# One step of a chunked RWKV-7 scan: four small products on the two column halves of TensorE

## The chip, the cores and the metric

The kernel runs on one core of a Trainium2 chip. The metric is the time of one execution on the device, in microseconds (us). Before the change the median of three executions is 3085.67 us. In the profile, PE is TensorE's products and PEld its weight loads, DVE is VectorE, ACT is ScalarE, POOL is GpSimd and SP the queue of SyncE, which here only issues transfers.

## The reference

The model is two layers. Each is a half-step feed-forward block, a mixer and a second half-step feed-forward block, at width 1024 over 528 tokens (16 learned tokens and 512 of the input). The mixer runs a convolution branch beside an RWKV-7 branch of 16 heads of size 64. The change lies in the recurrence of that branch, which the reference writes token by token:

```python
def _rwkv7_scan(r, decay, k, v, kk, a):
    B, L, H, N = r.shape
    ...
    def step(S, inp):
        r_t, w_t, k_t, v_t, kk_t, a_t = inp
        sa = jnp.einsum("bhvk,bhk->bhv", S, -kk_t)
        S = (S * w_t[:, :, None, :]
             + sa[..., None] * (kk_t * a_t)[:, :, None, :]
             + v_t[..., None] * k_t[:, :, None, :])
        y = jnp.einsum("bhvk,bhk->bhv", S, r_t)
        return S, y
    S0 = jnp.zeros((B, H, N, N), jnp.float32)
    _, ys = lax.scan(step, S0, xs)
    return jnp.moveaxis(ys, 0, 1)
```

## The kernel before, in words

**The chunked scan.** The 512 tokens are cut into eight chunks of 64 (`NCH` = 8, `C` = 64), and the 16 heads into four groups of four. `scan` (L1389) handles one group, with one pass of its loop for each chunk, so there are 2 x 4 x 8 = 64 scan steps in the program. Within a step the four heads h = 0 to 3 are handled side by side, and a step needs the state that the step before it left.

**One step.** Two transposes (L1404) bring the values of the chunk into rows 0 to 63 of the PSUM tile `tr`. ScalarE copies them into rows 0 to 63 of `sv` (L1405), whose rows 64 to 127 already hold the state, and into rows 0 to 63 of `va` (L1407). Four products (L1409), one for each head, take the whole 128 rows of `sv[:, h]` against 64 columns of `G`, the array that holds the masked scores above the decayed keys. They write 64 x 64 results side by side into columns 256 to 511 of `tr`, all in rows 0 to 63. ScalarE copies all four to `w` in one instruction of 64 x 256 (L1411). Then come two lists of products, head by head and in turn: L1418 multiplies `w` by the inverse that `inverse` put into `G`, into rows 64 to 127 of `ch`; L1421 multiplies the state by the decayed r, into rows 0 to 63. Each works on one 64 x 64 quarter of the array. ScalarE copies L1418's result to `va` (L1424), four products of 128 x 128 (L1426) add the chunk's contribution, VectorE makes the next state (L1432, L1433), and ScalarE stores the output rows (L1439).

**Passes.** Each product of float32 operands stands in the trace as two weight loads and two passes, so L1409's four products are eight passes in a step. The products of the large projections (L246, L217) use float32r and are one pass each.

**What stands around the step.** While the scan runs, the mixer lays other work between its parts: projections for later groups (L246, each weight block against two halves of the tokens), the scores of the next group (transposes L1250, products L1259 of 64 rows by 128 columns, L1236 of 64 rows by 16 columns), the inverse of the next half (L1333 and L1340, on quarters of the array), transposes and output work of the group before (L1528), and on VectorE the taps of the convolution (L1088). The order in which the code calls these is not the order in which they run: a scheduler takes the recorded instructions, their dependences and priorities, and its own estimates of durations, and writes one list for each engine. Each engine then works its list strictly in order, so a change of one group's shape shifts what stands behind it. A few lists are tied together by hand: `chain` in `scan` fixes the order of L1418, L1421 and L1426 among themselves.

Of the kernel before, what the change touches and what calls it, by code (L numbers as in the profile page):

```python
# [16 lines left out]
P = 128  # L17
# [13 lines left out]
C = 64  # L31
# [67 lines left out]
class Trunk:  # L99
# [1289 lines left out]
    def scan(self, q, Q):  # L1389


        nc, mp = self.nc, self.mp
        G, SB, pc, sv = Q["G"], self.sb, Q["pc"], Q["sv"]
        hc = lambda x: x.rearrange("p (h v) -> p h v", h=4)
        ysb = mp.tile([P, NCH * 4, 32], F32, name="b4", bufs=B4)
        ysb = ysb.rearrange("p a b -> p (a b)").rearrange("p (m h v) -> p m h v", m=4, h=4)
        Q["y"] = ysb
        for c in range(NCH):
            cs = slice(NM + c * C, NM + (c + 1) * C)
            left = lambda h: slice(h * HS, (h + 1) * HS)  # L1400
            right = lambda h: slice(256 + h * HS, 256 + (h + 1) * HS)
            tr = self.sm("tr")
            for p in range(2):
                nc.tensor.transpose(tr[0:C, p * P:(p + 1) * P], Q["v"][p][:, cs], self.ident)  # L1404
            nc.scalar.copy(sv[0:C], hc(tr[0:C, 0:256]))  # L1405
            va, w = (mp.tile([P, 4, HS], F32, name=x, bufs=n) for x, n in (("va", 2), ("w0", W0)))
            nc.scalar.copy(va[0:C], hc(tr[0:C, 0:256]))  # L1407
            for h in range(4):
                nc.tensor.matmul(tr[0:C, right(h)], G[:, h // 2, h % 2, 0, cs], sv[:, h, :],  # L1409
                                 start=True, stop=True)  # L1410
            nc.scalar.copy(w[0:C], hc(tr[0:C, 256:512]))  # L1411


            ch = self.sm("ch")
            chain = []
            rows = slice(0, P if c + 1 < NCH else C)
            for h in range(4):
                chain.append(nc.tensor.matmul(ch[C:P, left(h)], G[0:C, h // 2, h % 2, 1, cs],  # L1418
                                              w[0:C, h, :], start=h == 0, stop=True,
                                              skip_group_check=True))  # L1420
                chain.append(nc.tensor.matmul(ch[0:C, right(h)], G[HS:P, h // 2, h % 2, 1, cs],  # L1421
                                              sv[HS:P, h, :], start=h == 0, stop=False,
                                              skip_group_check=True))
            nc.scalar.copy(va[C:P], hc(ch[C:P, 0:256]))  # L1424
            for h in range(4):
                chain.append(nc.tensor.matmul(ch[rows, right(h)], SB[:, c, h, rows], va[:, h, :],  # L1426
                                              start=False, stop=True, skip_group_check=True))
            self.scanned = chain[-1]
            nsv = None
            if c + 1 < NCH:  # L1430
                nsv = self.new_state()
                nc.vector.tensor_tensor(nsv[HS:P], hc(ch[HS:P, 256:512]), sv[HS:P], op=ALU.add)  # L1432
                nc.vector.tensor_tensor(nsv[HS:P], nsv[HS:P],  # L1433
                                        pc[HS:P, :, c + 1:c + 2].to_broadcast([HS, 4, HS]),
                                        op=ALU.mult)
            for later, earlier in zip(chain[1:], chain):
                self.nosync(later, earlier)
            ro = C * (c % 2)
            nc.scalar.copy(ysb[ro:ro + C, c // 2], hc(ch[0:C, 256:512]))  # L1439
            sv = nsv  # L1440
            yield
# [317 lines left out]
```

## Time and profile before

| | |
|---|---|
| median of three executions | 3085.67 us (3079.16 to 3091.76) |
| the profiled execution | 3085.23 us |
| its span, first to last instruction | 3083.5 us |
| mean granted TensorE clock | 0.979 |
| scan steps, first and last copy to `w` | 64, from 622.6 to 2532.7 us |
| ScalarE busy | 1435.6 us (47%) |
| VectorE busy | 2277.9 us (74%) |

The page gives the busy time of each engine and a chain of work followed back from the last instruction. A row of a timeline has the start, the length, the engine, the line, the operation, what it writes and reads, and how many instructions were merged into the row. A row of a group has the count, the busy time and the mean duration, and then the idle time ahead of it and what ended that idle time. A row of waits has the waiting engine and line, what ended the wait, the total, the number of waits and the longest. The duration of a PE pass includes the way through the array, so what counts for throughput is the distance between starts, not the duration.

### The profile page before, as it was taken

The numbers are of one execution on the slowest core, as the hardware profiler recorded it, in microseconds if no ns is written. First come the engines' busy times: TensorE is split into PE (matmuls) and PEld (weight loads), VectorE is DVE, ScalarE is ACT, GpSimd is POOL, SyncE is SP. The second block draws the span as 40 slices with busy tenths as digits, with TensorE's granted clock in tenths as the row PEclk, the third lists the DMA queues.
The fourth block names the chain that finished last, engine by engine and source line by source line (L and its number), as shares of the span: only waits on it lengthen the run. The fifth ranks groups of instructions, "written<-read, shape, count | busy, mean of one in ns | idle before, by whom it ended". The sixth has DMA issues, their size and how long they took to land.

```text
span 3083.5 us, 64248 instructions
## 1 busy us (share of the span) xinstructions
PE 3009.6 (98%) x26140; PEld 2885.9 (94%) x26140; DVE 2277.9 (74%) x4689; ACT 1435.6 (47%) x2553; POOL 178.4 (6%) x286
## 2 busy tenths in 40 slices
PE   9999999999999999999999999999999999999998
PEld 9999999889988899999999999899889889999998
DVE  6766777897875768676776768778788757677767
ACT  4454454344454535444454544543354545254543
POOL 0110000000000000100000100000000000001100
PEclk9999999998999999999999999999899999999999
DMA  7665444334355554565556554444254645546651
GB/s 197 154 143 131 107 150 139 93 86 124 98 148 130 168 150 127 133 151 124 128 130 151 140 131 103 157 133 106 69 131 115 146 122 168 154 123 146 151 142 59
DMA packets 556149, 405.29 MB, mean 131 GB/s; under 512 B 89306, under 2 KB 500798, under 8 KB 555854
## 3 DMA queue, kind: packets, MB, share of 16 engines
q1 hardware_dynamic: 520302, 308.49, 34.9%
q0 software_dynamic: 30944, 84.18, 14.8%
q10 hardware_dynamic: 4608, 8.52, 0.8%
q8 instruction: 205, 3.36, 0.5%
q14 instruction: 90, 0.74, 0.1%
HBM read 270.81 MB, written 47.12 MB: 103 GB/s over the span
## 4 chain that ended last, share of the span: by engine, by line
PE 83%; DVE 7%; DMA 4%; ACT 3%; issue 2%; SPq 1%; ACTq 0%; DVEq 0%; POOLq 0%
PE mm L217 52%; PE mm L246 16%; PE sc L1340 2%; PE ch L1426 2%; PE tr L1409 1%; PE sc L1259 1%; PE ch L1418 1%; DMA w_raw<-in_w_in_dram 1%; DVE w_lo L160 1%; DVE cacc L1088 1%; ACT w_hi L149 1%; PE sc L1012 1%; DVE ln_rstd L444 1%; DMA w_lo<-w_raw 1%; PE sc L1144 1%
## 5 line engine op out<-in xcount | busy, mean ns | idle before, releaser
L217 PE MATMUL mm<-xh,w_hi 128*128 128x264 f32 (+1 forms) x1792 | 509.0, 285 | 7.6 <-ACT xh L460 5.7
L217 PE MATMUL mm<-xl,w_hi 128*128 128x264 f32 (+1 forms) x1792 | 507.8, 284 | 0.7 <-DVE xl L461 0.3
L217 PE MATMUL mm<-xh,w_lo 128*128 128x264 f32 (+1 forms) x1792 | 506.6, 283 | 0.0
L217 PE MATMUL mm<-hh,w_hi 128*128 128x264 f32 (+1 forms) x1408 | 400.4, 285 | 1.8 <-ACT hh L112 1.8
L217 PE MATMUL mm<-hh,w_lo 128*128 128x264 f32 (+1 forms) x1408 | 400.5, 285 | 0.0
L217 PE MATMUL mm<-hl,w_hi 128*128 128x264 f32 (+1 forms) x1408 | 400.1, 284 | 0.2
L246 PE MATMUL mm<-xh,w_lo 128*128 128x264 f32 x1760 | 390.3, 298 | 7.8 <-DMA w_lo<-w_raw 7.2
L246 PE MATMUL mm<-xh,w_hi 128*128 128x264 f32 x1760 | 385.8, 297 | 5.7 <-DVE kp L962 2.9
L246 PE MATMUL mm<-xl,w_hi 128*128 128x264 f32 x1760 | 385.0, 296 | 0.0
L1088 DVE SCALAR_TENSOR_TENSOR cacc<-cu,cw,cacc 128x528 f32<-128x528 f32 (+1 forms) x480 | 355.6, 752 | 4.3 <-ACT cacc L1086 0.6
L217 PEld LDWEIGHTS mm<-xh,w_hi 128*128 128x128 f32 x1792 | 335.9, 188 | 11.6 <-ACT xh L460 8.3
L217 PEld LDWEIGHTS mm<-xl,w_hi 128*128 128x128 f32 x1792 | 337.7, 189 | 2.7 <-DVE xl L461 2.5
L217 PEld LDWEIGHTS mm<-xh,w_lo 128*128 128x128 f32 x1792 | 337.5, 188 | 0.2 <-DVE w_lo L160 0.2
L122 ACT CAST w_hi<-sums 128x512 fp32r<-128x512 f32 (+1 forms) x204 | 154.7, 759 | 313.6 <-PE mm L217 202.1
L246 PEld LDWEIGHTS mm<-xh,w_lo 128*128 128x128 f32 x1760 | 285.0, 194 | 15.3 <-DMA w_lo<-w_raw 8.3
L246 PEld LDWEIGHTS mm<-xh,w_hi 128*128 128x128 f32 x1760 | 284.8, 194 | 12.1 <-DVE kp L962 3.2
L246 PEld LDWEIGHTS mm<-xl,w_hi 128*128 128x128 f32 x1760 | 283.8, 193 | 5.5
L217 PEld LDWEIGHTS mm<-hh,w_hi 128*128 128x128 f32 x1408 | 265.5, 189 | 2.4 <-ACT hh L112 2.0
L217 PEld LDWEIGHTS mm<-hl,w_hi 128*128 128x128 f32 x1408 | 265.7, 189 | 0.9 <-DVE hl L113 0.8
L217 PEld LDWEIGHTS mm<-hh,w_lo 128*128 128x128 f32 x1408 | 266.2, 189 | 0.1
L160 DVE TENSOR_TENSOR w_lo<-w_raw,w_hi 128x1024 fp32r<-128x1024 f32 (+1 forms) x194 | 204.1, 1054 | 80.8 <-ACT w_hi L149 72.1
L149 ACT CAST w_hi<-w_raw 128x1024 fp32r<-128x1024 f32 x134 | 140.4, 1049 | 240.3 <-PE mm L246 65.3
(364 smaller groups left out, 6847.1 us busy)
## 6 DMA issues: line engine op xcount, KB each, us to landing
w_raw<-in_w_in_dram SPq DMA_DIRECT2D x116, 512.0 KB
w_lo<-w_raw POOLq DMA_DIRECT2D x100, 512.0 KB, 5.0
w_raw<-in_ffn_wg_dram SPq DMA_DIRECT2D x88, 512.0 KB
w_raw<-in_ffn_wu_dram SPq DMA_DIRECT2D x88, 512.0 KB
w_raw<-in_ffn_wd_dram SPq DMA_DIRECT2D x80, 512.0 KB
w_lo<-w_raw POOLq DMA_DIRECT2D x68, 256.0 KB, 3.5
w_raw<-in_rwkv_wo_dram SPq DMA_DIRECT2D x16, 512.0 KB
w_raw<-in_conv_wo_dram SPq DMA_DIRECT2D x16, 512.0 KB
```

Of the source, the lines that this page charges most:

```text
L122: self.nc.scalar.copy(hi, x)
L149: copy = self.nc.scalar.copy(hi[:, :kt], raw[:, :kt])
L160: sub = self.nc.vector.tensor_tensor(lo[:, k], raw[:, k], hi[:, k].bitcast(F32), op=ALU.subtract)
L217: self.issued = self.nc.tensor.matmul(pm, a[:, k, :], b[:, xk + k, s], start=first and k == 0 and j == 0, stop=last and k == nk - 1 and j ...
L246: m = self.issued = nc.tensor.matmul(pm[:, h, :n], a[:, wk + k, :], b[:, xk + k, s:s + n], start=first and k == 0 and j == 0, stop=last an ...
L444: nc.vector.reciprocal(rstd[:, :n], rstd[:, :n])
L1012: nc.tensor.matmul(pm, w[a][r, o, :], x[b][r, s], start=j == 0, stop=j == 2)
L1088: tap = nc.vector.scalar_tensor_tensor(y, x, w, y, op0=ALU.mult, op1=ALU.add)
L1144: nc.tensor.matmul(tr[:, 32 * j:32 * j + 32], sq[:, k0:k0 + P], self.bones[:, ::4], start=True, stop=True)
L1259: pairs.append(nc.tensor.matmul(ps[:, e, p * P:(p + 1) * P], FB[p][r, fs], G[r, p, 1, :, cs], start=True, stop=True))
L1340: nc.tensor.matmul(ps[r, i, cs], vt[r, i], x[r, i, cs], start=True, stop=True)
L1426: chain.append(nc.tensor.matmul(ch[rows, right(h)], SB[:, c, h, rows], va[:, h, :], start=False, stop=True, skip_group_check=True))
```

## The change

The four products for `w` keep their operands. Heads 0 and 2 still write rows 0 to 63 of `tr`, now in columns 256 to 383; heads 1 and 3 write rows 64 to 127 of the same columns. The rows of the result are the columns of the array, so the even heads use its columns 0 to 63 and the odd heads its columns 64 to 127. The result for `w` then lies in two row halves, and the one copy to `w` becomes two, one for the even heads and one for the odd heads, each of 64 x 2 x 64. `w` itself is laid out as before. The two added lines shift all later line numbers by two, and the products stand at L1410 in place of L1409.

```diff
+            halves = [slice(0, C), slice(C, P)]
             for h in range(4):
-                nc.tensor.matmul(tr[0:C, right(h)], G[:, h // 2, h % 2, 0, cs], sv[:, h, :],
-                                 start=True, stop=True)
-            nc.scalar.copy(w[0:C], hc(tr[0:C, 256:512]))
+                nc.tensor.matmul(tr[halves[h % 2], right(h // 2)], G[:, h // 2, h % 2, 0, cs],
+                                 sv[:, h, :], start=True, stop=True)
+            for e, r in enumerate(halves):
+                nc.scalar.copy(w[0:C, e::2], tr[r, 256:384].rearrange("p (h v) -> p h v", h=2))
```

The scheduler lays the program out anew with this. TensorE's list in the seventh step of the first scan, before, from the products for `w` (L1409) to the first products that read it (L1418); `mm` is a projection and `sc` the next group's scores:

```order
L1409 MATMUL tr<-sv,G 64x64 x4
L246 MATMUL mm<-xh,w_lo 128x264
L246 MATMUL mm<-xh,w_hi 128x264
L1250 MATMUL sc<-ident,FB 128x128 x2
L246 MATMUL mm<-xh,w_hi 128x264
L246 MATMUL mm<-xl,w_hi 128x264
L1418 MATMUL ch<-w_7880,G 64x64
L1421 MATMUL ch<-sv,G 64x64
```

The same step on TensorE in the changed program, where the products for `w` are L1410 and their readers L1420, up to the second head of the readers:

```order
L1410 MATMUL tr<-sv,G 64x64 x4
L246 MATMUL mm<-xh,w_hi 128x264
L246 MATMUL mm<-xl,w_hi 128x264 x2
L1420 MATMUL ch<-w_7886,G 64x64
L1423 MATMUL ch<-sv,G 64x64
L1250 MATMUL sc<-ident,FB 128x128
L1420 MATMUL ch<-w_7886,G 64x64
L1423 MATMUL ch<-sv,G 64x64
```

Fewer rows stand between the products for `w` and their first reader, three projection passes in place of four and two transposes, and a transpose now stands between head 0 and head 1 of the readers.

ScalarE's list around the copies for `w` in the second step of the first scan, before; `b` is the output tile and `va` the operand of the step's last products:

```order
L1439 COPY b_7414<-ch 64x256
L1407 COPY va<-tr 64x256
L1411 COPY w_7559<-tr 64x256
L1424 COPY va<-ch 64x256
L1405 COPY sv<-tr 64x256
```

The same place on ScalarE in the changed program:

```order
L1441 COPY b_7414<-ch 64x256
L1407 COPY va<-tr 64x256
L1413 COPY w_7560<-tr 64x2x64 x2
L1426 COPY va<-ch 64x256
L1405 COPY sv<-tr 64x256
```

The two copies stand next to each other where the one stood, and nothing is laid between them.

## The prediction

> **What bounds the kernel now.** I began with the page, for the engine that has no room, and went on to the stretches in which the scan runs.
>
> ```profile
> PE 3009.6 (98%) x26140; PEld 2885.9 (94%) x26140; DVE 2277.9 (74%) x4689; ACT 1435.6 (47%) x2553; POOL 178.4 (6%) x286
> ...
> PE 83%; DVE 7%; DMA 4%; ACT 3%; issue 2%; SPq 1%; ACTq 0%; DVEq 0%; POOLq 0%
> ```
>
> TensorE is busy for 98% of the span and carries 83% of the chain that ended last. The stretches of the two mixers, one row each (TensorE, its weight loads, VectorE, ScalarE, GpSimd, then the granted clock and the share of the DMA engines), say the same of the place of the change:
>
> ```profile
> 400.00:1020.00 620.00, 598.05 (x5800) 548.12 (x5801) 477.58 (x1169) 289.10 (x576) 24.86 (x61) 0.96 0.47 124
> 1930.00:2545.00 615.00, 597.09 (x5709) 546.66 (x5709) 468.81 (x1106) 285.50 (x567) 21.66 (x57) 0.95 0.46 123
> ```
>
> Of 1235 us, TensorE is busy for 1195. So a scan step is not a bare chain of waits: the list fills its gaps with projections. A change in a step is therefore worth what it does to the number of slots on TensorE, and a longer wait within the step costs only where nothing fills it. The groups that the change touches, by shape, and what TensorE's loads wait for at these lines:
>
> ```profile
> L1409 PE MATMUL tr<-sv,G 128*64 128x64 f32 x512 | 45.6, 234 | 7.4 <-DVE sv L1433 4.4 <-ACT va L1407 2.2
> ```
>
> ```profile
> L1411 ACT COPY w<-tr 64x256 f32<-64x256 f32 x64 | 23.3, 365 | 39.7 <-PE tr L1409 39.2
> ```
>
> ```profile
> PEld tr L1409 <- ACT b L1439: 6.2, 14, 1.7
> ...
> PEld ch L1418 <- ACT w L1411: 3.8, 11, 0.6
> ...
> PEld tr L1409 <- ACT va L1407: 3.5, 5, 1.4
> ...
> PEld tr L1409 <- DVE sv L1433: 1.4, 3, 0.6
> ```
>
> The copies' 39.7 us of idle time ahead of them is ScalarE's and costs nothing. What counts is that TensorE waited for `w` at only 11 of 64 steps, 3.8 us in all, and ahead of the products for `w`, at L1409, 6.2 + 3.5 + 1.4 = 11.1 us in 22 waits. One step late in the second layer, first TensorE's rows and then the row of its copy:
>
> ```profile
> 2526.34 0.40 PE L246 MATMUL mm<-xh,w_hi 128*128 128x264 f32 x2
> 2526.57 0.41 PE L246 MATMUL mm<-xl,w_hi 128*128 128x264 f32 x2
> 2526.91 0.68 PE L1409 MATMUL tr<-sv,G 128*64 128x64 f32 x8
> 2527.51 0.51 PE L246 MATMUL mm<-xh,w_lo 128*128 128x264 f32 x2
> 2527.86 0.41 PE L246 MATMUL mm<-xh,w_hi 128*128 128x264 f32 x2
> 2528.20 0.27 PE L1418 MATMUL ch<-w,G 64*64 64x64 f32 x1
> 2528.21 0.27 PE L1421 MATMUL ch<-sv,G 64*64 64x64 f32 x1
> ...
> 2528.66 0.22 PE L1418 MATMUL ch<-w,G 64*64 64x64 f32 x1
> 2528.66 0.22 PE L1421 MATMUL ch<-sv,G 64*64 64x64 f32 x1
> ```
>
> ```profile
> 2527.62 0.37 ACT L1411 COPY w<-tr 64x256 f32<-64x256 f32 x1 [0.81 <-PE tr L1409]
> ```
>
> **The change part by part.**
>
> *The products in pairs.* The eight passes of L1409 take 0.68 us, of which the last pass's own length is about 0.22 (as the last rows of L1418 and L1421 have it), so their starts lie over 0.68 - 0.22 = 0.46 us. The eight passes of L1418 and the eight of L1421 start from 2528.20 to 2528.66, over the same 0.46 us: twice the passes in the same time, because the two lists work on different quarters of the array. If the odd heads run beside the even ones in the same way, L1409's eight passes need four slots of 0.46 / 8 = 0.058 us fewer, 0.23 us a step, and 64 x 0.23 = 14.7 us in all. L1418 and L1421 differ in their rows of the array as well as in their columns, while the two halves here share all rows. Another place shows products that share rows. At 758 us the inverse's products, which work with rows 0 to 63 on columns 0 to 63 and with rows 64 to 127 on columns 64 to 127, run among L1418 and L1421, which use the other two quarters:
>
> ```profile
> 758.22 0.22 PE L1418 MATMUL ch<-w,G 64*64 64x64 f32 x1
> 758.23 0.22 PE L1340 MATMUL sc<-b 64*64 64x32 f32 x1
> 758.23 0.22 PE L1421 MATMUL ch<-sv,G 64*64 64x64 f32 x1
> 758.28 0.22 PE L1340 MATMUL sc<-b 64*64 64x32 f32 x1
> 758.28 0.22 PE L1418 MATMUL ch<-w,G 64*64 64x64 f32 x1
> 758.28 0.22 PE L1340 MATMUL sc<-b 64*64 64x32 f32 x1
> 758.28 0.22 PE L1421 MATMUL ch<-sv,G 64*64 64x64 f32 x1
> ```
>
> L1418 starts at 758.22 and again at 758.28, its usual 0.06 us apart, although L1340 starts passes on the same rows in between. So sharing rows did not hold the passes apart. No row has two products of all 128 rows on two column halves, so I keep both ends, 14.7 us and nothing, and take 14.7, since the nearest rows overlap fully. The Trainium skill speaks against this: "TensorE: Matmul & The Clock Gate", Part 3 on packing small matmuls, under the mechanism, says that a weight load overlaps running products only where their row groups differ. By that rule the odd heads' loads would wait for the even heads' passes and this term would be zero; the rows at 758 us, of quarters, do not bear it out.
>
> *The second copy.* A copy of 128 elements a row is shown by a scale vector's copy on ScalarE, with what started behind it:
>
> ```profile
> 722.87 0.29 ACT L1154 COPY rx<-rs 16x128 f32<-16x128 f32 x1
> 723.07 0.69 ACT L960 ACTIVATE e<-mm,tm 128x528 f32<-128x528 f32 x1
> ```
>
> It takes 0.29 us, and the next one starts 0.20 us after it. In place of one copy of 0.37, the even heads' ends 0.37 - 0.29 = 0.08 us earlier and the odd heads' ends 0.20 + 0.29 - 0.37 = 0.12 us later. Head 0 of the readers needs the first, head 1 the second. In the step shown, L1409's last pass starts at 2527.37, the copy runs from 2527.62 to 2527.99, and four projection passes hold TensorE until 2528.20, 0.21 us after `w` was there: the 0.12 is hidden. Where that cover is gone it costs 0.12, at the 11 waits of today 1.3 us, and at most 64 x 0.12 = 7.7 us. I take 1.3. Queued behind the second copy on ScalarE stands the copy to `va` (L1424), which waits for the readers of `w` anyway, and 64 more issues of 0.20 us are 13 us on an engine that is 47% busy.
>
> *The new lists.* Since head 0 is now ready before head 1, the scheduler lays other work between them. Counted over the two programs, 7 of 64 steps had something between the eight readers before, and 33 have it now; in 7 and 31 of them it is work of another shape of the array. What such a detour costs is shown where L1259 stood between the readers:
>
> ```profile
> 2331.53 0.22 PE L1418 MATMUL ch<-w,G 64*64 64x64 f32 x1
> 2331.53 0.22 PE L1421 MATMUL ch<-sv,G 64*64 64x64 f32 x1
> 2331.68 0.49 PE L1259 MATMUL sc<-G,FB 64*128 64x128 f32 x2
> 2332.10 0.27 PE L1418 MATMUL ch<-w,G 64*64 64x64 f32 x1
> ```
>
> From 2331.53 to 2332.10 are 0.57 us where two readers stand 0.06 apart, so the detour takes 0.51. Its two passes start at most 0.49 - 0.27 = 0.22 apart (0.27 being the length of a first pass), and would need at most as much elsewhere, so at least 0.29 is the price of changing shape and back. If they need half of that, it is 0.40. I take 0.35, and 31 - 7 = 24 more detours make 24 x 0.35 = 8.4 us. The ends are zero, if TensorE would have waited there for the odd heads' copy, and 24 x 0.51 = 12.2 us. The other moves in the lists, the few transfers of SP and the few rows of POOL among them, have no sign that the trace can tell; the change itself issues no transfer and passes none.
>
> *The sum.* -14.7 + 1.3 + 8.4 = -5.0 us. The profiled execution took 3085.23 us, its span 3083.5 and 1.7 around it; it stands 0.4 below the median of the runs. So 3085.2 - 5.0 = 3080.2, and I say 3080. A difference of under 0.5%, 15.4 us, is about what a measurement of this kernel cannot tell from no change, and the first term alone is smaller than that.
>
> Beside this stands a figure of the Trainium skill: the same page and part gives a measured speedup of 2.38 for three column tiles. As an estimate, 2.38 / 3 of two is 1.59, which would cut 0.46 us by 0.17 a step and 10.9 in all, and the sum would be -1.2 us; no run here shows it.
>
> **The rivals.**
>
> *All of the gain, and more.* The detours fall into time in which TensorE would have waited, and the step, 0.23 us shorter, also takes from the 22 waits ahead of L1409, 22 x 0.23 = 5.1 us of their 11.1. For it speaks that the list was laid for the earlier head 0. Against it speak 0.21 us of slack in the step shown: TensorE was not waiting there, so a detour there is paid in full. It gives -14.7 - 5.1 = -19.8 us, 3065 us.
>
> *The halves do not run side by side.* Then the change does not do what it says: eight slots stay, the detours and the copy's 1.3 us are paid, and it is +9.7 us, 3095 us. The rows at 758 us speak against it; that they are quarters and not halves speaks for it. The rule quoted above would end here.
>
> *The step's own chain becomes the bound, and the kernel is slower.* The place is TensorE's list between L1410 and the readers of `w`. It now has fewer passes there (three projections where four and two transposes stood, in the step shown with the change), the odd heads come 0.12 us later, a detour adds 0.51 between head 0 and head 1, and in the first step of the second scan 44 projection passes of about 0.12 us (0.23 for two, from 2526.34 to 2526.57) now stand between head 0 and head 1, 5.3 us. If the chain sets the time in the mixer it loses 31 x 0.51 + 64 x 0.12 + 5.3 = 28.8 us and wins only 14.7 minus what the thinner filling leaves open, one pass of 0.12 us a step, 7.7 us. That is 28.8 - 7.0 = +21.8 us, 3107 us. It is slower by over 0.5% from a loss of 15.4 + 7.0 = 22.4 us on, which is when the waits at the readers, 3.8 us today, and the detours together reach about 26. Against it speaks that the passes taken out here stand elsewhere in the list and fill other gaps.
>
> **How the numbers follow.** The forecast of 3080 has 0.58; its own range takes the detours from 0 to 12.2 us and the copy from 0 to 7.7, so from 3085.2 - 14.7 = 3070.5 to 3085.2 - 14.7 + 12.2 + 7.7 = 3090.4, all within 0.5%. All of the gain has 0.18, and is the chance of faster by over 0.5%. No pairs has 0.12, at 3095 still within 0.5% (the limit is 3085.2 + 15.4 = 3100.6). The chain has 0.12, of which 0.10 is slower by over 0.5% and 0.02 falls short of it. Within 0.5% there are 0.58 + 0.12 + 0.02 = 0.72. The range goes from 3065 to 3096: it leaves out the chain and the lower part of the first rival, about 0.2.
>
> **What would show it.** Right: L1410's busy time falls from 45.6 us to about 45.6 - 14.7 = 31, its passes start in pairs 0.06 us apart, a step's eight in about 0.23 us; two copies of about 0.29 us start 0.20 apart; readers in two parts, with about 0.5 us between them, at some 31 steps; waits at the readers under 8 us. Wrong: L1410 still over 0.46 us a step (no pairs), waits and detours at the readers of 26 us or more (the chain), or a gain or loss of over 10 us outside the two mixer stretches, where nothing changes.

## The result and the profile after

The changed kernel takes 3100.24 us in the median of 6 runs (3092.63 to 3106.03), the kernel before 3081.72 us in 6 runs beside it (3079.16 to 3091.76). The ratio is 1.0052, with a 95% interval of 1.0028 to 1.0076. A later group of runs gave 3100.12 against 3083.98 us, 1.0059 [1.0038, 1.0080]. So the change costs about half a per cent. The prediction said 3080 us, with a range up to 3096, and was wrong.

The profiled execution took 3102.7 us. Its page, TensorE first, and then the shares of the chain that ended last:

```profile
PE 3014.8 (97%) x26140; PEld 2886.5 (93%) x26140; DVE 2277.8 (73%) x4689; ACT 1447.6 (47%) x2617; POOL 178.5 (6%) x286
...
PE 82%; DVE 7%; DMA 5%; ACT 3%; issue 2%; SPq 1%; ACTq 0%; DVEq 0%; POOLq 0%
```

The two mixer stretches, the same windows as before:

```profile
400.00:1020.00 620.00, 597.04 (x5749) 544.07 (x5747) 476.41 (x1167) 292.13 (x604) 21.56 (x56) 0.95 0.46 122
1930.00:2545.00 615.00, 588.41 (x5660) 537.98 (x5660) 470.33 (x1104) 290.82 (x594) 20.71 (x55) 0.96 0.45 120
```

TensorE is busy for 1185.45 of the 1235 us where it was busy for 1195.14, and gets 51 + 49 = 100 fewer passes started in them. It did less in the same time: its idle time in the two windows went from 39.9 to 49.6 us. Over the whole span, the span less TensorE's busy time on the page is 3083.5 - 3009.6 = 73.9 us before and 3101.0 - 3014.8 = 86.2 us after. ScalarE's 28 and 27 instructions more are mostly the second copies. Now the products themselves, grouped by shape:

```profile
L1410 PE MATMUL tr<-sv,G 128*64 128x64 f32 x512 | 29.9, 236 | 5.2 <-ACT va L1407 2.2 <-DVE sv L1435 2.0
```

Their busy time fell from 45.6 to 29.9 us. So the pairs do run side by side, as predicted (31). One step late in the second layer, first TensorE's rows and then the copies:

```profile
2539.06 0.45 PE L1410 MATMUL tr<-sv,G 128*64 128x64 f32 x8
2539.44 0.40 PE L246 MATMUL mm<-xh,w_hi 128*128 128x264 f32 x1
...
2540.16 0.28 PE L246 MATMUL mm<-xh,w_hi 128*128 128x264 f32 x1
2540.37 0.27 PE L1420 MATMUL ch<-w,G 64*64 64x64 f32 x1
```

```profile
2539.60 0.56 ACT L1413 COPY w<-tr 64x128 f32<-64x128 f32 x2
```

The eight passes take 0.45 us in place of 0.68. The two copies together take 0.56 where one took 0.37. Each alone takes 0.26, as the row of all of them shows (shortest, median and longest in ns, then when the first and the last started):

```profile
L1413 ACT COPY w<-tr x128: 238/263/278, 625.5 to 2550.0; 64x128 f32<-64x128 f32 x128
```

So the second starts about 0.28 us after the first and not 0.20: they do not overlap. Over the 64 steps two copies end 0.55 us after the first one's start against 0.37, 0.18 us later, where 0.12 was predicted. The waits of TensorE's loads around the step:

```profile
PEld mm L246 <- DMA w_lo<-w_raw: 11.9, 7, 5.3
...
PEld ch L1428 <- ACT va L1426: 7.6, 13, 3.6
...
PEld ch L1420 <- ACT w L1413: 3.8, 11, 0.5
...
PEld tr L1410 <- ACT va L1407: 3.1, 3, 1.4
PEld tr L1410 <- ACT b L1441: 3.1, 12, 0.4
...
PEld tr L1410 <- DVE sv L1435: 0.6, 1, 0.6
```

TensorE waits for `w` exactly as long as before, 3.8 us in 11 waits. The waits ahead of the products fell from 11.1 us to 3.1 + 3.1 + 0.6 = 6.8. Waits elsewhere grew: for `va` ahead of the step's last products from 3.0 to 7.6 us (3.6 of it in one wait), and for a transfer of weights from 8.3 to 11.9, as the rows of before show:

```profile
PEld mm L246 <- DMA w_lo<-w_raw: 8.3, 6, 3.3
...
PEld ch L1426 <- ACT va L1424: 3.0, 8, 0.8
```

**The clock and the time.** The mean granted clock of the profiled execution is lower than in the one before (0.979):

```profile
core 0: 3101.0 us, clock 0.977
```

That matters here. The 113 runs of the kernel before that stand beside the experiments below spread from 3071 to 3102 us, and their clocks from 0.974 to 0.985. One straight line through the runs of every kernel below, each kernel with its own level, gives 2.68 us for each 0.001 of clock and leaves a scatter of 2.5 us. Below, "at equal clock" is a kernel's level on that line minus that of before, with a 95% interval. The mean of before is 3086.1 us at 0.9795, that of the changed kernel in 15 runs 3100.6 us at 0.9763. So its loss of 14.5 us is 3.2 x 2.68 = 8.6 us of clock and 6.1 +- 1.4 us at equal clock (the sum differs by rounding). In the profiled executions the program ends 17.5 us later. Of that, 2.8 us are there when the first mixer's projections start, ahead of any changed instruction, and about 6 in all lie outside the mixers, where the lists do the same work. The two mixers take the other 11.5 us.

### The profile page after: what moved, and what is told of

It reads as the page before. It is cut to its first block, busy times and chain, and to the rows that moved or that the text cites. A ratio compares the mean times of both kernels' runs of the same rounds, so it can differ in the third digit from the quotient of the medians.

```text
span 3101.0 us, 64307 instructions
## 1 busy us (share of the span) xinstructions
PE 3014.8 (97%) x26140; PEld 2886.5 (93%) x26140; DVE 2277.8 (73%) x4689; ACT 1447.6 (47%) x2617; POOL 178.5 (6%) x286
## 3 DMA queue, kind: packets, MB, share of 16 engines
q0 software_dynamic: 30944, 84.18, 14.7%
## 4 chain that ended last, share of the span: by engine, by line
PE 82%; DVE 7%; DMA 5%; ACT 3%; issue 2%; SPq 1%; ACTq 0%; DVEq 0%; POOLq 0%
PE mm L217 52%; PE mm L246 16%; PE sc L1340 2%; PE ch L1428 2%; PE sc L1259 1%; PE ch L1420 1%; DMA w_lo<-w_raw 1%; DMA w_raw<-in_w_in_dram 1%; DVE w_lo L160 1%; SPq L1308 1%; PE tr L1410 1%; DVE ln_rstd L444 1%; PE sc L1012 1%; DMA a<-ascr 1%; ACT w_hi L149 1%
## 5 line engine op out<-in xcount | busy, mean ns | idle before, releaser
L246 PE MATMUL mm<-xh,w_hi 128*128 128x264 f32 x1760 | 392.1, 300 | 6.3 <-DVE kp L962 2.9
L246 PEld LDWEIGHTS mm<-xh,w_lo 128*128 128x128 f32 x1760 | 286.5, 196 | 18.8 <-DMA w_lo<-w_raw 11.9
```

What stands on the lines that cost most here:

```text
L246: m = self.issued = nc.tensor.matmul(pm[:, h, :n], a[:, wk + k, :], b[:, xk + k, s:s + n], start=first and k == 0 and j == 0, stop=last an ...
```

## The experiments

Fifteen kernels, in the groups in which they ran. The ratio is to the kernel before in the same group. The last column is the span less TensorE's busy time in the one profiled execution of each, 73.9 us for the kernel before.

| kernel | median us, before | ratio, interval | mean clock | at equal clock | TensorE idle, us |
|---|---|---|---|---|---|
| changed kernel, again | 3100.12, 3083.98 | 1.0059 [1.0038, 1.0080] | 0.9763 (15 runs) | +6.1 +- 1.4 | 83.3 |
| e1: two copies, no pairs | 3093.22, 3086.57 | 1.0019 [0.9999, 1.0039] | 0.9797 | +8.0 +- 1.5 | 76.9 |
| e2: changed, odd heads read first | 3088.04, 3086.57 | 0.9999 [0.9975, 1.0022] | 0.9776 | -2.0 +- 1.5 | 85.3 |
| e3: e1, odd heads read first | 3107.24, 3086.57 | 1.0057 [1.0034, 1.0080] | 0.9757 | +8.4 +- 1.5 | 81.2 |
| e4: before, another list | 3089.29, 3086.57 | 1.0006 [0.9985, 1.0028] | 0.9787 | +1.0 +- 1.5 | 78.1 |
| g1: before, whole copy twice | 3089.09, 3083.98 | 1.0015 [0.9999, 1.0031] | 0.9817 | +8.3 +- 1.5 | 73.7 |
| g2: pairs, one copy | 3093.59, 3083.98 | 1.0041 [1.0018, 1.0065] | 0.9766 | +1.9 +- 1.5 | 90.0 |
| g4: e2, second copy on VectorE | 3113.40, 3083.98 | 1.0099 [1.0072, 1.0126] | 0.9732 | +10.2 +- 2.1 | 91.1 |
| h1: changed, another list | 3103.90, 3083.73 | 1.0064 [1.0039, 1.0089] | 0.9765 | +10.4 +- 2.1 | 83.0 |
| h2: e2, another list | 3082.94, 3083.73 | 0.9995 [0.9973, 1.0016] | 0.9789 | -4.4 +- 1.5 | 83.2 |
| h3: before, products twice | 3112.70, 3083.73 | 1.0095 [1.0070, 1.0119] | 0.9825 | +35.9 +- 2.1 | 66.9 |
| h4: e2, pairs twice | 3105.67, 3083.73 | 1.0064 [1.0042, 1.0087] | 0.9790 | +16.1 +- 1.5 | 80.8 |
| k1: products of two heads alone | 3075.33, 3089.81 | 0.9967 [0.9948, 0.9987] | 0.9804 | -6.9 +- 1.5 | 80.6 |
| k2: k1, another list | 3093.69, 3089.81 | 1.0020 [1.0002, 1.0038] | 0.9784 | +3.3 +- 1.5 | 79.2 |
| k3: g2, another list | 3077.89, 3089.81 | 0.9970 [0.9946, 0.9993] | 0.9796 | -5.4 +- 1.5 | 77.7 |

"Another list" is SC_LATE at 52 in place of 50. It is a constant at line 58 by which the scores of the next group are put back in the scheduler's order, and moving it lays the same work in another list. "Changes" below are changes of the array's shape from one row of TensorE's list to the next, 634 before and 680 in the changed program. "Split steps" have something between the eight readers of `w`, 7 before and 33 in the changed program.

### First group: is it the copies, the detours, or any new list?

**e1_copies.** The copy to `w` in two parts, and nothing else:

```diff
-            nc.scalar.copy(w[0:C], hc(tr[0:C, 256:512]))
+            for e in range(2):
+                nc.scalar.copy(w[0:C, e::2], hc(tr[0:C, 256:512])[:, e::2])
```

> The products for w as before the change, all into rows 0 to 63 and one after another; only the copy to w is made in two, even heads and odd heads. TensorE's list then has something between the readers of w at 29 of 64 steps (7 before, 33 with the change). Theory A (the second copy makes the scheduler split the readers of w, and the array's changes of shape and the waits that come with it eat what the pairs win): no pairs, all of the loss, so slower than before by about the change's 18 us and the pairs' 15 us together, 25 to 33 us, ratio about 1.009. Theory B (any new list loses against the one before, by waits for transfers that happen to collide): anywhere from 0 to +20 us. Theory C (the column halves themselves cost something, in TensorE or in reading rows 64 to 127): about before, within 5 us.

It loses 8.0 us at equal clock, without any pairs: the split copy alone moves the list (684 changes, 29 steps with split readers). That is far from the 25 to 33 us of theory A. What its copies show, though, is quicker than in the changed kernel:

```profile
2527.23 0.40 ACT L1412 COPY w<-tr 64x128 f32<-64x128 f32 x2
...
2532.21 0.42 ACT L1412 COPY w<-tr 64x128 f32<-64x128 f32 x2 [1.05 <-PE tr L1409]
```

Two copies of 0.26 end within 0.42, so the second starts 0.16 us after the first.

**e2_odd_first.** The changed kernel with the readers in the order 1, 0, 3, 2, so that the first reader needs the copy that comes last and nothing is laid between them:

```diff
-            for h in range(4):
+            for h in (1, 0, 3, 2):
...
-                                              w[0:C, h, :], start=h == 0, stop=True,
+                                              w[0:C, h, :], start=h == 1, stop=True,
```

> The changed kernel, with the readers of w taken in the order of heads 1, 0, 3, 2. The first reader then needs the second copy, and nothing is ready early to be split off: 7 steps with other shapes between the readers, as before the change. Theory A: the pairs' 15.7 us stay and the odd heads' copy costs 1 to 3 us, so 10 to 15 us faster than before, ratio 0.995 to 0.997, and L1410 busy about 30 us. Theory B: as the change, 5 to 20 us slower than before. Theory C: as the change, about 18 us slower.

Its list has 10 split steps in place of 33 and 634 changes, as many as before. At equal clock it is 8.1 us faster than the changed kernel. That is near the 8.4 us that the prediction gave the detours. But it is only 2.0 us faster than before and not the 10 to 15 of theory A, although its pairs run side by side (30.0 us busy). TensorE waits for `w` and `va` more than in the changed kernel:

```profile
PEld ch L1428 <- ACT va L1426: 9.4, 16, 3.5
...
PEld ch L1420 <- ACT w L1413: 6.4, 19, 0.8
```

**e3_copies_odd_first.** Both edits at once, e1 with the readers' order of e2, so two copies without pairs and almost without split steps (8; 661 changes).

> No pairs (products for w as before), two copies, and readers in the order of heads 1, 0, 3, 2: 6 steps with other shapes between the readers. Theory A: near before, +2 to +8 us, and some 15 us behind e2_odd_first, which is the value of the pairs alone. Theory B: 5 to 20 us slower than before, and no steady distance to e2_odd_first. Theory C: near before, and faster than e2_odd_first.

+8.4 us at equal clock, 10.4 more than e2, which has the pairs. The readers' order thus brought nothing here: e1 loses 8.0 us with 23 changes more. Its clock, 0.9757, is as low as that of the changed kernel, without any pairs.

**e4_relay.** The kernel before with its list laid anew:

```diff
-SC_LATE = 50
+SC_LATE = 52
```

> The kernel before the change with one number of the scheduler's priorities moved (the scores' priority 52 in place of 50), nothing else: the same instructions in a new list, with 2 steps split in place of 7. It shows what laying the list anew does by itself. Theory A: within 6 us of before, either way. Theory B: slower than before by 10 us or more.

+1.0 us with 620 changes. A new list is not in itself a loss.

### Second group: does the step's chain set the time?

**g1_copy_twice.** Before, with one line more, the whole copy to `w` made a second time:

```diff
             nc.scalar.copy(w[0:C], hc(tr[0:C, 256:512]))
+            nc.scalar.copy(w[0:C], hc(tr[0:C, 256:512]))
```

> The kernel before the change, with the copy to w made twice, the whole of it each time: no product is added or moved in the code, but w is ready about 0.27 us later in each of 64 steps (the distance of two such copies in the trace of before). TensorE's list has 677 changes of array shape in place of 634. Theory D (the scan's step is a chain of dependent parts, and what counts is the time round that chain, not TensorE's slots): 64 x 0.27 = 17 us, and about 43 x 0.25 = 11 for the changes of shape, 28 us in all. Theory S (TensorE's slots count, and a later w is hidden by the passes laid behind it): the changes of shape alone, about 11 us, or less.

**g2_one_copy.** The pairs with one copy of 128 rows in place of two; it leaves out the odd heads' recurrence:

```diff
-            for e, r in enumerate(halves):
-                nc.scalar.copy(w[0:C, e::2], tr[r, 256:384].rearrange("p (h v) -> p h v", h=2))
+            nc.scalar.copy(w[:, 0:2], tr[:, 256:384].rearrange("p (h v) -> p h v", h=2))
...
-                                              w[0:C, h, :], start=h == 0, stop=True,
+                                              w[0:C, h // 2, :], start=h == 0, stop=True,
```

> The changed kernel with one copy of 128 rows by 128 elements in place of the two: both row halves of the result go to w as they lie, and the readers of the odd heads take the even heads' rows, so that the recurrence of the odd heads is not computed. It has the pairs and no second copy; 645 changes of shape. Theory D: the step's chain is shorter by 0.23 (pairs) and by about 0.1 (a copy of 128 elements in place of 256), 64 x 0.33 = 21 us, less 11 x 0.25 = 3 for shapes: about 18 us faster than before, ratio 0.994. Theory S: the pairs' 15 less 3, 12 us faster.

**g4_two_engines.** e2 with the odd heads' copy on VectorE:

```diff
-                nc.scalar.copy(w[0:C, e::2], tr[r, 256:384].rearrange("p (h v) -> p h v", h=2))
+                (nc.scalar.copy, nc.vector.tensor_copy)[e](w[0:C, e::2], tr[r, 256:384].rearrange("p (h v) -> p h v", h=2))
```

> The changed kernel with readers in the order of heads 1, 0, 3, 2, and the odd heads' copy on VectorE, so that the two copies run beside each other. 675 changes of shape. Theory D: the copies end 0.2 us earlier in a step than with both on ScalarE, unless VectorE is in the middle of a tap (0.75 us each): somewhere from 10 us faster to 15 us slower than before, and the waits of TensorE for w tell which. Theory S: the pairs' 15 less 10 for the shapes, about 5 us faster.

**c_after.** The changed kernel, unedited, in this group.

> The changed kernel once more, beside the others on one chip, to tell its loss from that of the granted clock. In the runs so far the time falls by about 2.8 us for each 0.001 of mean granted clock, in every kernel. Theory D and theory S: 5 to 18 us slower than before, and about 5 us slower than before at the same clock.

g1 makes the way from the products to `w` 0.4 us longer at every step (copies of 0.37 us that start 0.40 apart or more). If that way set the time, it would cost 64 x 0.4 = 25.6 us. It costs 8.3, with 43 more changes, near theory S and far from the 28 us of theory D. g2 makes the same way shorter:

```profile
2527.65 0.26 ACT L1412 COPY w<-tr 128x128 f32<-128x128 f32 x1
```

`w` is there 0.26 us after the copy starts in place of 0.55, and the pairs are in; it is still 1.9 us slower than before at equal clock, where theory D had a gain of 18 us and theory S one of 12. Its TensorE is idle for 90.0 us. So the step's chain through `w` does not set the time, and in this list it is not the second copy that ate the gain of the pairs. g4 was meant to run the copies beside each other and did not: VectorE's copy, which writes the same tile, starts after the end of ScalarE's in all 64 steps, and in 20 of them VectorE waited for it.

```profile
L1413 DVE COPY w<-tr x64: 267/293/295, 631.2 to 2561.0; 64x128 f32<-64x128 f32 x64
...
  ACT w L1413: 14.0, 20
```

It lost 10.2 us and says nothing on two engines.

### Third group: what is a slot worth?

**h1_after_relay** is the changed kernel and **h2_odd_relay** is e2, each with SC_LATE at 52, the edit of e4.

> The changed kernel with the scheduler's constant SC_LATE at 52, so that the same work is laid in another list: 691 changes of the array's shape on TensorE against 680 in the changed kernel and 634 before, 31 steps with split readers. If the loss belongs to the change (changes of shape at about 0.16 us each, pairs worth about 4 us): 0.16 x 57 - 4 = +5 us against before at equal clock, as the changed kernel's own +6. If the loss is the luck of one list: anything from -6 to +12, and not near +6.

> The changed kernel with the odd heads' readers first, and SC_LATE at 52: 630 changes of shape, 9 split steps. Changes of shape at 0.16 us and pairs worth 4: -0.6 - 4 = -5 us against before at equal clock. If pairs are worth their slots: -12 to -15 us. If the list's luck decides: unlike the -2 of the same kernel at 50 by more than 5 us either way.

+10.4 and -4.4 us at equal clock, where the same kernels had +6.1 and -2.0. Both lists of the changed kernel lose and both with the other order gain a little, so the loss goes with the change and its readers' order and not with one unlucky list. h1 stands 5 us above what was expected, though: in these two pairs of lists the luck of a list is 2 to 4 us.

**h3_products_twice** is before, **h4_pairs_twice** is e2, each with its products issued a second time over the first:

```diff
-            for h in range(4):
+            for h in (0, 1, 2, 3) * 2:
```

> The kernel before with the products for w issued twice (the second time over the first, the same values): eight more slots a step, 0.46 us, 29.4 us in all, and 696 changes of shape. If slots on TensorE count in full: 29.4 + 62 x 0.16 = +39 us. If slots at this place count for a third, as the pairs seemed to: 10 + 10 = +20 us. If waits hide them: +10 us.

> The changed kernel with the odd heads' readers first and the products issued twice in pairs: as many slots as before the change, four more a step than with single pairs (14.7 us), 677 changes of shape. Against the same kernel with single pairs (-2 us at equal clock): slots in full 14.7 + 43 x 0.16 = +21.6 us, so about +20 against before; slots for a third 5 + 7 = +12, so about +10; waits hide them +7, so about +5. If pairs lower the granted clock, its mean clock is under 0.976; if not, about 0.979.

One step of h4, sixteen passes in pairs:

```profile
2528.50 0.69 PE L1410 MATMUL tr<-sv,G 128*64 128x64 f32 x16
```

Sixteen passes in pairs take 0.69 us, and eight without pairs took 0.68: a pair takes one slot. h3 lost 35.9 us, close to the 39 for slots that count in full. h4 is 18.1 us behind e2 and 20.5 behind h2, close to 21.6. With 0.18 us for a change of shape (the fit below) taken out, eight slots more in h3 cost 24.7 of 29.4 us, and four more in h4 cost 10.4 (against e2) and 12.0 (against h2) of 14.7. So slots added at this place cost 70 to 84% of their time, and four fewer, in e2 and h2, brought 2.0 and 4.4 us of 13.7.

### Fourth group: does a slot freed without pairs count?

**k1_two_heads.** Before with the products of heads 0 and 1 alone, four passes and no pairs; it leaves out the recurrence of heads 2 and 3:

```diff
-            for h in range(4):
+            for h in range(2):
...
-            nc.scalar.copy(w[0:C], hc(tr[0:C, 256:512]))
+            nc.scalar.copy(w[0:C, 0:2], tr[0:C, 256:384].rearrange("p (h v) -> p h v", h=2))
...
-                                              w[0:C, h, :], start=h == 0, stop=True,
+                                              w[0:C, h % 2, :], start=h == 0, stop=True,
```

> The kernel before with the products for w of heads 0 and 1 alone: four passes a step in place of eight, on one column half and without pairs, one copy of 64x128, and the readers of heads 2 and 3 take the values of heads 0 and 1, so that the recurrence of heads 2 and 3 is not computed. 641 changes of shape on TensorE against 634. As many slots are freed as by the pairs. If freed slots count here and the pairs have a hidden price of their own: -14.7 + 7 x 0.19 = -13 us against before at equal clock, more by the shorter copy. If freed slots turn into waits whatever frees them: 0 to -4 us, as the odd-heads-first kernels with pairs.

**k2_two_heads_relay** is k1 and **k3_one_copy_relay** is g2, each with SC_LATE at 52.

> The same with SC_LATE at 52, another drawing of the list: 680 changes of shape. If freed slots count: -14.7 + 46 x 0.19 = -6 us. If they turn into waits: -2 + 8.7 = +5 to +9 us.

> Pairs with one copy of 128 rows (the odd heads' readers take the even heads' rows, so the odd heads' recurrence is not computed), with SC_LATE at 52: 658 changes of shape. At 50 it was +2 with 645. If the second copy is what eats the pairs' gain: below -8 us here. If not, and a change costs 0.19: +2 + 13 x 0.19 = +4.5 us.

The four passes of k1 in two steps:

```profile
2511.58 0.45 PE L1409 MATMUL tr<-sv,G 128*64 128x64 f32 x4
...
2521.03 0.42 PE L1409 MATMUL tr<-sv,G 128*64 128x64 f32 x4 [1.30 <-DVE sv L1433]
```

They take the 0.45 us of the eight passes in pairs, and a shorter copy follows. k1 gains 6.9 us at equal clock, about half of what its slots were worth by the prediction's price and between the two expected figures; k2, with 39 more changes than k1, loses 3.3, near the +5 that stood for waits. k3 gains 5.4 where the same edit in g2 lost 1.9, with 13 changes more, against what was expected. With the changes of shape taken out at 0.18 us, the freed slots bring 8.2 us in k1, 5.0 in k2, 0.1 in g2 and 9.7 in k3. So without pairs too (k1, k2) a freed slot counts for a third to a half, and what one list makes of it varies by up to 10 us (g2, k3). A hidden price of the pairs of a few us is neither shown nor excluded: without pairs -6.9 and +3.3, with pairs and one copy +1.9 and -5.4.

The idle time of TensorE tells where a part of the freed slots went. In the nine kernels of the table that free slots it is 77.7 to 91.1 us, 83.7 in the mean, and in the six others 66.9 to 81.2, 76.3 in the mean, against 73.9 before. That is one execution of each, and the two groups overlap, but in the mean the kernels that free some 14 us of slots have about 7 us more of idle time than those that do not.

## Why the prediction was wrong

**The pairs: right in the trace, wrong as a gain.** In the steps that ran at full clock, the weight loads of the eight passes start over 0.403 us before (57 steps) and over 0.189 on average in the changed kernel (62 steps). That is 0.214 x 64 = 13.7 us of slots, against 14.7 predicted. The rule of the Trainium skill that spoke against it ("TensorE: Matmul & The Clock Gate", Part 3, the mechanism: a weight load overlaps running products only where the row groups differ) does not hold for these products. The two halves share all 128 rows, and the busy time fell from 45.6 to 29.9 us. The rival in which the halves do not run side by side falls with it.

The step that failed stands under what bounds the kernel: "A change in a step is therefore worth what it does to the number of slots on TensorE, and a longer wait within the step costs only where nothing fills it." The first half of that sentence holds for the most part for slots that are added (h3, h4) and not for slots that are freed (e2, h2, g2, k1, k2). The order of the list is fixed before the run. When one group gets shorter, TensorE comes earlier to the next entry, and if that entry's operand is late for another reason, the time becomes a wait. The idle time shows it: it grew by 12.3 us in the changed kernel (73.9 to 86.2), by 11.4 in e2 and 9.3 in h2. No single row shows it: waits for `va` grew from 3.0 us to 7.6 in the changed kernel and 9.4 in e2, but e1, which frees no slot, has 6.7 of them:

```profile
PEld ch L1427 <- ACT va L1425: 6.7, 10, 4.1
```

The second step that failed is the clock, for which the sum had no term: it took the granted clock as unchanged without a word, and the clock is what carried the time past 3096 us (below).

**The second copy: mis-sized, and its cover held.** It ends 0.18 us later and not 0.12, because the copies do not overlap. TensorE's waits for `w` stayed at 3.8 us in 11 waits, so it cost nothing there, as the prediction said of its cover. What a second copy costs elsewhere is the fit's 3.5 us below, which no row shows.

**The detours: about right.** A split step of the changed kernel:

```profile
914.47 0.22 PE L1420 MATMUL ch<-w,G 64*64 64x64 f32 x1
914.48 0.22 PE L1423 MATMUL ch<-sv,G 64*64 64x64 f32 x1
914.63 0.39 PE L246 MATMUL mm<-xh,w_lo 128*128 128x264 f32 x1
914.94 0.27 PE L1420 MATMUL ch<-w,G 64*64 64x64 f32 x1
```

From 914.47 to 914.94 are 0.47 us where two readers stand 0.06 apart, for one pass that takes 0.12 in its own company: a price of 0.29 us, below the 0.35 taken. Undoing them in e2 gave back 8.1 us at equal clock, h2 against h1 14.8, with 46 and 61 fewer changes. The sum gave 8.4. Without pairs the same order gave nothing back (e3 against e1), so the agreement in e2 is in part luck.

**The sum, again.** A least-squares fit over the table and before, an estimate and no more (the changed kernel is one of its 16 points), gives, with one standard error, 0.18 +- 0.04 us for a change, 0.36 +- 0.10 of its time for a freed slot, 0.84 +- 0.15 for an added one and 3.5 +- 1.8 us for a second copy, and leaves a scatter of 3.4 us. For the changed kernel that is 46 x 0.18 - 0.36 x 13.7 + 3.5 = +6.9 us, against +6.1 measured. The prediction had 8.4 - 14.7 + 1.3 = -5.0. Nearly all of the difference of 11 is the pairs' term, which should have been about -5.

**The clock: not in the sum.** It is 8.6 of the 14.5 us. With clocks as before, the time would have stood at about 3086 + 6 = 3092 us, within the range of the prediction. The lower clock goes with the program and not with the chip: in the group of c_after, on one chip, the nine runs of the changed kernel have 0.9763 in the mean and the 26 of the kernel before 0.9804. In the two mixer windows of the profiled execution it stands at 0.95 and 0.96, as before (0.96 and 0.95). What in the changed program lowers it stays open. Kernels with pairs stand from 0.9732 to 0.9796 and kernels without from 0.9757 to 0.9825. e3 is low without pairs, and h4, with twice as many pairs, is at 0.9790, so pairs alone do not decide it.

**The chain as the bound** was the rival on the slower side. The sign was its own, the mechanism not: waits for `w` did not grow, g1 lengthens that way by 0.4 us a step at a third of the price, and g2 shortens it for nothing.

**All of the gain, and more** was the rival on the faster side. The waits ahead of the products did fall by 4.3 us where it said 5.1, but the idle time as a whole grew.

**What stays open.** Which operand bounds the mixers once slots are freed. The waits that grew differ from list to list (`va`, `w`, the transfer of weights), and a wait for a transfer or another engine has not been tried by itself. No kernel that computes the reference is shown to be faster than before; h2 comes nearest, with -4.4 +- 1.5 us at equal clock and a ratio of 0.9995 [0.9973, 1.0016].

## What to carry over

A TensorE that is busy for 97% of the span does not make a freed slot worth its time: where the order is fixed, look at what the next entry waits for, and expect a part of the slot back, while an added slot is paid for the most part. When one result is split in two, try letting the first reader take the part that is ready last, so that the scheduler lays no foreign work between the readers: it gave 8 and 15 us with pairs, and nothing without. Before a difference of half a per cent is explained, compare at equal granted clock.

## What the runs showed of the hardware

**Two copies on ScalarE overlapped where both kept to one row half.** In e1 both copies read rows 0 to 63 of `tr` and write rows 0 to 63 of `w`, and the second starts 0.16 us after the first (0.26 + 0.16 = 0.42 for both). In the changed kernel the second reads rows 64 to 127 into rows 0 to 63 and starts 0.28 us after the first, which is longer than the first takes. In neither list does the second copy wait for anything of its own. The overlap of 0.10 us in e1 agrees with the Trainium skill ("ScalarE: Activation LUTs", what ACT_TABLE_LOAD costs), which gives about 93 ns for successive ACTIVATE instructions; the changed kernel shows that it can be missing.

The trace of before already has both cases. The output copy L1439 reads rows 0 to 63 and writes rows 64 to 127 of the output tile in odd chunks, rows 0 to 63 in even ones. Here it stands behind L1407, which keeps to rows 0 to 63, first in an odd chunk and then in an even one:

```profile
903.75 0.36 ACT L1407 COPY va<-tr 64x256 f32<-64x256 f32 x1
904.14 0.37 ACT L1439 COPY b<-ch 64x256 f32<-64x256 f32 x1
...
908.83 0.36 ACT L1407 COPY va<-tr 64x256 f32<-64x256 f32 x1
909.10 0.37 ACT L1439 COPY b<-ch 64x256 f32<-64x256 f32 x1
```

It starts 0.39 us after L1407 in the odd chunk and 0.27 in the even one. Wherever the two stand back to back the same holds, in 6 odd chunks and 11 even ones. So the prediction could have read from this trace that a copy with rows of the other half need not overlap; its row of L1154 did not show that case.

**Products of all 128 rows pair on the two column halves.** Eight passes in 0.45 us against 0.68, sixteen in 0.69.

**With each 0.001 of granted clock the time of this kernel moves by 2.7 us,** and with no edit at all it goes from 3071 to 3102 us, a spread of 1%, twice the effect that was studied.
